# The pair of tiles that GpSimd stores: tiles 8 and 15 behind its second turn, or tiles 0 and 7 behind its first

## The chip, the cores and the metric

The kernel runs on one core of one Trainium2 chip. A core has five engines with instruction streams of their own (TensorE, VectorE, ScalarE, GpSimd, SyncE, in the profile PE, DVE, ACT, POOL, SP) and sixteen DMA engines. The metric is the time of one execution on the device in microseconds, as the median of several runs.

## The reference

```python
# x: (16, 512, 1024), weight: (1024, 768), add_value: (16, 512, 768), all float32; scale: 0.1
return (scale * np.matmul(x, weight) + add_value).astype(np.float32)
```

Flattened, this is one product of 8192 x 1024 by 1024 x 768, scaled, with an 8192 x 768 matrix added. The core reads x (32 MB), the weights (3 MB) and the added matrix (24 MB) and writes 24 MB.

## The kernel before

**Tiles and slots.** The 8192 rows are 64 tiles of 128 rows. Partition p of a block of 16 tiles holds 16 consecutive rows of the matrix, one for each tile, so that several tiles of one block are one contiguous piece of memory in each partition. x is loaded into `xs`, which has 16 slots of a tile each. `ao` has 32 slots: a tile of the added matrix is loaded there, the result overwrites it, and it is stored from there. Tile t uses slot t modulo 32, so tiles 32 to 39 can be loaded only when tiles 0 to 7 have been stored.

**Moving and turning.** ScalarE and GpSimd run the same program, `mover`: each casts half of every group of four tiles from `xs` to bfloat16 in one of two buffers `va` (L167, eight casts of 32 partitions for four tiles and engine). One turn of its loop is the 16 tiles of `xs`, so there are four turns, of 32 casts each. For each of them it waits until the x tiles have landed and until VectorE has transposed what was in that buffer. VectorE transposes two tiles at a time from `va` to `xt` (L182), TensorE multiplies (L214), and VectorE scales the product, adds `ao` and writes the result to `ao`, again for two tiles (L191). VectorE's loop `group` takes eight tiles in a turn. Its semaphore `made` counts finished tiles (above a constant `MADE`), `by_act` and `by_pool` count the casts of ScalarE and GpSimd.

**SyncE's order.** All other transfers are issued by SyncE from a list written by hand, `STREAM`: entries (kind, first tile, number of tiles), with "w" for weights, "x" for x, "a" for the added matrix, "o" for a store, "a+" for a wait for an added load, and "pair" for the pair's rows. `sync_engine` goes through it in order and waits before each entry for what it needs: an x load (L116) for the casts that free its slots, an added load (L129) for the added load before it and, from tile 32 on, for the store that frees its slots, a store (L147) for the results. They all go to one queue, q1 in the profile. The last store, of tiles 60 to 63, stands behind the list (L257).

**The pair.** Two tiles of one block of eight are not stored with the others. 122 of their 128 partitions are stored by GpSimd in three DMAs (`BY_POOL`: partitions 117 to 121, 0 to 104 and 105 to 116), and the last six, 122 to 127, by SyncE (`BY_SP`), all at L93. GpSimd's DMAs go to a queue of their own, q0 in the profile. GpSimd issues them between two parts of its `mover`: after `TURN_AT` turns it waits for the results, issues the three DMAs and goes on with the other turns:

```python
mover(nc.gpsimd, nc.gpsimd.tensor_copy, 1, by_pool, pool_go, 0, TURN_AT)
nc.gpsimd.wait_ge(made, MADE + PAIR.stop)
for p, n in BY_POOL:
    store_pair(nc.gpsimd, p, n, aside_sem)
mover(nc.gpsimd, nc.gpsimd.tensor_copy, 1, by_pool, pool_go, TURN_AT, T // X_SLOTS - TURN_AT)
```

The added load that reuses the first of the pair's slots waits for both of the pair's semaphores, `pair_sem` and `aside_sem`.

Of the kernel before, what the change touches and what calls it, by code (L numbers as in the profile page):

```python
# [21 lines left out]
STREAM = [  # L22
# [5 lines left out]
]  # L28
FIRST, LAST = (0, 8), (60, 4)
PAIR, TURN_AT = slice(8, 16, 7), 2  # L30
BY_SP, BY_POOL = [(122, 6)], [(117, 5), (0, 105), (105, 12)]


# [259 lines left out]
```

## Time and profile before

| | us |
|---|---|
| median of 3 runs | 208.49 |
| lowest and highest | 208.33, 208.66 |
| the profiled execution | 209.46 |
| its span, from the first to the last instruction | 207.7 |

The profile is of one execution. Its span leaves out 1.76 us that lie around the instructions, and the whole took 0.97 us longer than the median. Rows of the timeline give start, duration, engine, line, operation and tiles, how many instructions were drawn together, and in brackets the idle time before and what ended it. Rows of DMA issues give the size and the median time from issue to landing. "DMA share" is the busy share of the sixteen DMA engines together.

### The profile page before, as it was taken

Reading aid. Unit: us, or ns where it says so; the run is one execution under the profiler, and the core shown is the slowest. Engines: PE = TensorE matmul, PEld = TensorE weight load, DVE = VectorE, ACT = ScalarE, POOL = GpSimd, SP = SyncE. Lnnn points to the kernel's source line nnn. Section 1 sums busy time; section 2 is a strip of 40 time slices with the busy share of each in tenths; the row PEclk is TensorE's granted clock in tenths of the full one; section 3 lists DMA queues with packets and bytes.
Section 4 is the critical chain, followed back from the end, with each engine's and each line's share of the span. In section 5 each row is a group of like instructions: output and inputs, shape, how many; then the busy total and the mean of one; then the engine's idle time right before and its main releaser. Section 6 shows DMA issues by size and latency. Waiting matters only on the chain.

```text
span 207.7 us, 2223 instructions
## 1 busy us (share of the span) xinstructions
PE 167.7 (81%) x1008; PEld 50.4 (24%) x512; DVE 98.0 (47%) x66; ACT 134.7 (65%) x129; POOL 137.7 (66%) x135
## 2 busy tenths in 40 slices
PE   0000099999999999999999999999999997999800
PEld 0000023333333333333333333323332232333200
DVE  0005525537555555475555553855551934455310
ACT  2049970799999708999997069999990299900000
POOL 0049994799999907999999359999991199910000
PEclk9999999999999999999999999999999999999975
DMA  7999999999999999999999999999999999998983
GB/s 297 410 380 473 417 447 404 454 454 404 404 454 454 404 448 454 380 426 414 445 419 449 407 451 454 404 428 436 445 431 417 423 447 450 454 454 381 447 379 166
DMA packets 4067, 87.04 MB, mean 419 GB/s; under 512 B 476, under 2 KB 476, under 8 KB 1122
## 3 DMA queue, kind: packets, MB, share of 16 engines
q1 hardware_dynamic: 3874, 86.28, 97.1%
q0 software_dynamic: 192, 0.75, 0.9%
q14 instruction: 1, 0.01, 0.0%
HBM read 61.87 MB, written 25.17 MB: 419 GB/s over the span
## 4 chain that ended last, share of the span: by engine, by line
PE 36%; DMA 29%; POOL 18%; ACT 5%; issue 4%; DVE 3%; SPq 0%; POOLq 0%; DVEq 0%; ACTq 0%
PE mm L214 36%; POOL va L167 17%; DMA xs<-in_x_dram 15%; DMA out_dram<-ao 14%; ACT va L167 5%; DVE xt L182 2%; POOL out_dram L93 1%; DVE ao L191 1%; SPq L129 0%; SPq L116 0%; DVEq L180 0%; POOLq L160 0%; POOLq L162 0%; POOLq L157 0%; DVEq L191 0%
## 5 line engine op out<-in xcount | busy, mean ns | idle before, releaser
L214 PE MATMUL mm<-w_bf,xt 128*128 128x256 bf16 (+1 forms) x1008 | 167.7, 327 | 28.6 <-DVE xt L182 27.7
L167 POOL CAST va<-xs 32x1024 bf16<-32x1024 f32 x128 | 135.5, 1059 | 44.8 <-DMA xs<-in_x_dram 37.4
L167 ACT CAST va<-xs 32x1024 bf16<-32x1024 f32 x128 | 133.4, 1043 | 46.0 <-DMA xs<-in_x_dram 43.0
L191 DVE SCALAR_TENSOR_TENSOR ao<-mm,ao 128x1536 f32 (+1 forms) x32 | 56.2, 1757 | 72.8 <-PE mm L214 68.2
L212 PEld LDWEIGHTS <-xt 128*128 128x128 bf16 x512 | 50.4, 98 | 145.4 <-issue 116.2
L182 DVE STREAM_TRANSPOSE xt<-va 128x1024 f32<-128x1024 f32 x32 | 39.5, 1236 | 9.2 <-POOL va L167 7.1
L175 DVE CAST w_bf<-ao 128x3072 bf16<-128x3072 f32 x2 | 4.5, 2251 | 18.2 <-DMA ao<-in_weight_dram 18.2
L156 ACT ACT_TABLE_LOAD x1 | 1.3, 1283 | 1.3 <-SPq L246 1.3
L93 POOL DMA_DIRECT2D out_dram<-ao x3 | 2.0, 662 | 0.0
L274 POOL MEMSET const-float32-0.0<- 128x1 f32 x1 | 0.1, 98 | 0.2 <-issue 0.2
L274 POOL MEMSET const-bfloat16-1.0<- 128x1 bf16 x1 | 0.1, 101 | 0.0
L274 POOL MEMSET const-float32-1.0<- 128x1 f32 x1 | 0.1, 98 | 0.0
L274 POOL MEMSET const-uint8-127<- 128x1 uint8 x1 | 0.1, 98 | 0.0
## 6 DMA issues: line engine op xcount, KB each, us to landing
xs<-in_x_dram SPq DMA_DIRECT2D x7, 4096.0 KB, 22.3
ao<-in_add_value_dram SPq DMA_DIRECT2D x6, 3072.0 KB, 16.1
out_dram<-ao SPq DMA_DIRECT2D x3, 3072.0 KB, 29.1
ao<-in_add_value_dram SPq DMA_DIRECT2D x1, 6144.0 KB, 24.2
out_dram<-ao SPq DMA_DIRECT2D x1, 6144.0 KB, 31.8
out_dram<-ao SPq DMA_DIRECT2D x1, 4608.0 KB, 15.3
xs<-in_x_dram SPq DMA_DIRECT2D x2, 2048.0 KB, 21.0
ao<-in_weight_dram SPq DMA_DIRECT2D x2, 1536.0 KB, 16.9
```

The lines of the kernel that those rows point to most:

```text
L93: eng.dma_start(out_v[p:p + n, 0, PAIR, :], ao[p:p + n, PAIR, :]).then_inc(sem, 16)
L156: eng.preload_act_table(mybir.ActivationFunctionType.Copy)
L167: copy(va[q % VA_BUFS][32 * b:32 * b + 32, :, a, :], src[32 * a:32 * a + 32, :, b, :]).then_inc(count, 1)
L175: eng.tensor_copy(w_bf[:, s:s + n, :], ao[:, W_AT + s:W_AT + s + n, :]).then_inc(casts, n)
L182: eng.transpose(xt[:, 2 * half:2 * half + 2, :, :].rearrange("p i c m -> p (i c m)"), va[move % VA_BUFS][:, q:q + 2 * KC, :, :].bitcast(fp ...
L191: eng.scalar_tensor_tensor(a, mm[:, q:q + 2, 0:N], float(scale), a, op0=mybir.AluOpType.mult, op1=mybir.AluOpType.add).then_inc(made, 2)
L212: eng.ldweights(x_j, tile_position=(0, 0))
L214: m = eng.add_instruction(mybir.InstMatmult(start_tensor_calc=(j == 0), stop_tensor_calc=(j == KJ - 1), tile_size=(P, P), tile_position=(0 ...
L274: nc = _bacc.Bacc("TRN2", target_bir_lowering=False, num_devices=1)
```

## The change

Three constants change, no function:

```diff
 STREAM = [
...
-    ("x", 32, 8), ("a+", 16, 16), ("o", 0, 8), ("o", 9, 6), ("pair", 8, 8), ("a", 32, 8), ("x", 40, 8),
+    ("x", 32, 8), ("a+", 16, 16), ("pair", 0, 8), ("o", 1, 6), ("o", 8, 8), ("a", 32, 8), ("x", 40, 8),
...
-PAIR, TURN_AT = slice(8, 16, 7), 2
+PAIR, TURN_AT = slice(0, 8, 7), 1
```

The pair is now tiles 0 and 7. GpSimd's first part is one turn (tiles 0 to 15) instead of two, it then waits for tile 7 instead of tile 15, issues the same three DMAs, and does the other three turns. SyncE stores the pair's last six partitions first, then tiles 1 to 6, then tiles 8 to 15, where it stored tiles 0 to 7, then 9 to 14, then the pair's six partitions. The waits on the pair's two semaphores move from the added load of tiles 40 to 47 to that of tiles 32 to 39. The bytes, the sizes of the DMAs and their partitions are the same. GpSimd's first part has three register instructions less, as a loop of one turn has constants to wait for; the other engines' instructions are unchanged.

## The prediction

> **What bounds the kernel now.** I read the page first: the totals by engine, the 40 slices, and the queues.
>
> ```profile
> span 207.7 us, 2223 instructions
> PE 167.7 (81%) x1008; PEld 50.4 (24%) x512; DVE 98.0 (47%) x66; ACT 134.7 (65%) x129; POOL 137.7 (66%) x135
> DMA  7999999999999999999999999999999999998983
> DMA packets 4067, 87.04 MB, mean 419 GB/s; under 512 B 476, under 2 KB 476, under 8 KB 1122
> q1 hardware_dynamic: 3874, 86.28, 97.1%
> q0 software_dynamic: 192, 0.75, 0.9%
> ```
>
> TensorE looks like the busiest engine at 81%, but the DMA row is 9 in nearly every slice, and SP's queue (q1) and GpSimd's queue (q0) together fill 98.0% of the sixteen DMA engines' span. So I asked for stretches, for the time around the change and behind it (the last two columns are the DMA share and the rate):
>
> ```profile
> core 0: us, PE busy (x) PEld busy (x) DVE busy (x) ACT busy (x) POOL busy (x), PEclk, DMA share, GB/s
> 55.00:79.00 24.00, 23.84 (x147) 7.19 (x75) 13.73 (x10) 16.47 (x17) 16.80 (x18) 1.00 0.99 427
> 96.00:116.00 20.00, 19.90 (x123) 5.97 (x61) 11.42 (x8) 16.55 (x16) 18.92 (x20) 1.00 1.02 437
> 116.00:198.00 82.00, 78.24 (x474) 23.48 (x240) 44.20 (x30) 50.05 (x48) 49.77 (x48) 1.00 1.00 430
> ```
>
> The DMA engines are full in the stretch where GpSimd's stores run now (96 to 116), in the one where they would run (55 to 79) and in all that follows. The rate is not lower where the two queues share the engines: 437 GB/s against 427 and 430. The end of the kernel is therefore the bytes divided by the rate, as long as the queue never runs empty. Then I looked at the end itself, with SP's issues in order of time and the DMA engines' last 2 us (slices of 0.05 us):
>
> ```profile
> 160.44 27.70 SPq L147 DMA_DIRECT2D out_dram<-ao  x2
> 198.45 0.33 SPq L257 DMA_DIRECT2D out_dram<-ao  x1
> out_dram<-ao SPq DMA_DIRECT2D x1, 1536.0 KB, 8.3
> GB/s 0 0 0 0 0 0 246 0 0 0 0 0 0 0 0 246 0 0 0 0 0 0 0 0 246 0 0 0 0 0 0 0 0 0 0 0 0 0 0 0
> DMA packets 8, 0.04 MB, mean 18 GB/s; under 512 B 5, under 2 KB 5, under 8 KB 5
> ```
>
> The last store (L257) is issued at 198.45 and lands 8.3 us later, at 206.7. Its 1.57 MB at 430 GB/s need 3.7 us, so some 4.6 us of it are the queue ahead of it and latency, which this row doesn't part; I take a little under half, 2 us, as the slack that TensorE's end still has. In the last window, 204.7 to 206.7, only three data packets of 12 KB start, 0.46 us apart: one of the sixteen DMA engines is finishing alone, 1.5 us after the others. Both facts come back below.
>
> **The change part by part.** The profiled execution took 209.46 us with a span of 207.7 us; the median of three runs is 208.49 us, 0.97 us less. I make the sum on the span and carry its difference to the median.
>
> GpSimd's three stores move from behind its second turn to behind its first. Its rows and SP's issues:
>
> ```profile
> 37.63 35.04 POOL L167 CAST va<-xs 32x1024 bf16<-32x1024 f32 x32 [4.21 <-DMA xs<-in_x_dram]
> 78.92 17.49 POOL L167 CAST va<-xs 32x1024 bf16<-32x1024 f32 x16 [6.24 <-DMA xs<-in_x_dram]
> 96.36 1.98 POOL L93 DMA_DIRECT2D out_dram<-ao  x3
> 98.39 17.48 POOL L167 CAST va<-xs 32x1024 bf16<-32x1024 f32 x16
> 121.42 8.72 POOL L167 CAST va<-xs 32x1024 bf16<-32x1024 f32 x8 [5.55 <-DMA xs<-in_x_dram]
> 55.21 17.88 SPq L116 DMA_DIRECT2D xs<-in_x_dram  x2
> 73.27 0.82 SPq L147 DMA_DIRECT2D out_dram<-ao  x2
> 74.14 0.38 SPq L93 DMA_DIRECT2D out_dram<-ao  x1
> 96.00 0.36 SPq L129 DMA_DIRECT2D ao<-in_add_value_dram  x1
> 96.49 0.85 SPq L116 DMA_DIRECT2D xs<-in_x_dram  x1
> 115.23 0.33 SPq L129 DMA_DIRECT2D ao<-in_add_value_dram  x1
> 115.94 0.33 SPq L116 DMA_DIRECT2D xs<-in_x_dram  x1
> 48.86 1.76 DVE L191 SCALAR_TENSOR_TENSOR ao<-mm,ao 128x1536 f32 x1 [1.13 <-PE mm L214]
> ```
>
> 1. GpSimd's new wait. Tiles 8 to 15 are the first half of the run that starts at 37.63, so the first turn ends at 37.63 + 17.5 = 55.1. The wait is for tile 7, and VectorE finishes tiles 6 and 7 at 48.86 + 1.76 = 50.6, the fourth result of its first group. The wait costs nothing; the 1.98 us of issue do: casts of tiles 16 to 23 end at 74.7 instead of 72.7.
>
> 2. Who waits for that. SP loads x tiles 32 to 39 when GpSimd has moved tile 23; that issue (the second of the two from 55.21, which end at 73.1), and the pair and the stores behind it in SP's order, go 1.98 us later, to 74.7. The x load before it is still running until 78.9, so the queue has 4 us of work left and nothing idles: 0 us. If it were empty, this would cost 1.98 us.
>
> 3. The bytes of q0 come earlier. The three DMAs carry 732 KB:
>
> ```profile
> out_dram<-ao POOLq DMA_DIRECT2D x1, 630.0 KB, 15.1
> out_dram<-ao POOLq DMA_DIRECT2D x1, 72.0 KB, 17.3
> out_dram<-ao POOLq DMA_DIRECT2D x1, 30.0 KB, 7.5
> ao<-in_add_value_dram SPq DMA_DIRECT2D x6, 3072.0 KB, 16.1
> 87.77 1.25 DVE L182 STREAM_TRANSPOSE xt<-va 128x1024 f32<-128x1024 f32 x1 [0.75 <-POOL va L167]
> 90.46 1.76 DVE L191 SCALAR_TENSOR_TENSOR ao<-mm,ao 128x1536 f32 x1 [1.45 <-PE mm L214]
> ```
>
> That is 0.75 MB; at 427 GB/s, 1.75 us that lie ahead of the landing of x tiles 24 to 31. Casts of tile 24 then start at 80.7 instead of 78.9. The transpose of tiles 24 and 25, at 87.77 now, already waits for GpSimd; it moves to 89.5 and ends at 90.8. TensorE needs it when tile 23 is done, just before VectorE's 90.46. So TensorE gets a stall of about 0.4 us that it does not have now. If the DMA engine that is last brings 1 of its 1.5 us to this place too, it is 1.4 us. From below the term is 0, if most of q0's packets still stand behind that x load.
>
> The Trainium skill bears on that last point: DMA: Bandwidth & Descriptors, Queues, rings and completion order, says that a DMA engine alternates between its queues packet by packet. The rows fit it: 192 packets, 12 per engine, took 15 to 17 us to land where their bytes need 1.75 us. By that rule q0's packets would alternate with the packets of a 6144 KB load, twice as long, so that an estimate from it is some 25 us instead of 17 for the landing, and up to a third of the 1.75 us would fall behind the x load. The stall would then be 0 to 0.4 us, and the sum the same.
>
> 4. Where the stall goes. TensorE's own gaps:
>
> ```profile
> 26.09 137.03 PE L214 MATMUL mm<-w_bf,xt 128*128 128x512 bf16 x819 [26.09 <-DVE xt L182]
> 163.35 10.57 PE L214 MATMUL mm<-w_bf,xt 128*128 128x512 bf16 x63 [0.24 <-DVE xt L182]
> 175.32 20.98 PE L214 MATMUL mm<-w_bf,xt 128*128 128x512 bf16 x126 [1.40 <-DVE xt L182]
> 160.39 1.76 DVE L191 SCALAR_TENSOR_TENSOR ao<-mm,ao 128x1536 f32 x1 [4.62 <-DMA ao<-in_add_value_dram]
> ```
>
> It idles 0.24 and 1.40 us late in the run, and VectorE waits 4.62 us for an add load there: DMA sets the pace. A stall of 0.4 to 1.4 us at tile 24 only shortens these 1.64 us. Behind that stand the 2 us of slack at the end. So 0 us.
>
> 5. GpSimd's second turn no longer issues, which gives the 1.98 us back: casts of tile 32 follow those of tile 31 at once, 80.7 + 17.5 = 98.2 against 98.39 now, and end at 115.7. The x load that SP issues at 115.94 for it stays there. The x load at 96.49 waits for tile 31 and goes to 98.2, where the store of tiles 8 to 15 keeps the queue full for some 4 us. 0 us.
>
> 6. SP's order. Ahead of the add load at 96.00 stood one store of 3072 KB; now 36 + 732 + 2304 = 3072 KB stand there, so it is issued at the same time. It now carries the waits on both pair semaphores, but q0's packets, issued from 55.1 to 57.1, land near 74 with the 17.3 us of now and have until 96. The next add load, at 115.23 now, waits today for GpSimd's 72 KB DMA (issued as the last of three, at 97.8, landing 17.3 us later, at 115.1). That wait goes; the next one is the landing of the add load before it, near 96.0 + 16.1 = 112. The load is issued 3 us earlier but stands behind an x load that lands at 121.4 either way: 0 us.
>
> Bytes, packet sizes and rate are unchanged, the queue is never empty, and both stalls are covered. The sum is 0.0 us: **208.5 us**.
>
> **The rivals.** First, faster: the engine that ends alone. One engine of sixteen has 1.5 us more work, and the pair's rows are the only transfer that isn't spread evenly by size; the slow landing of q0 and the pair's DMAs on the same engines are a place where it could pick that up. If it meets them at another point and half of the lag disappears, the end is 0.7 us earlier: 207.8 us. If all of it does, 207.0. For it speaks that this tail alone sets the end; against it, that the same rows go to the same queues in the same shares.
>
> Second, slower: the same engine falls further behind. If its lag of 1.5 us at 206.4 grows with the time since GpSimd issued its stores (96.4, so 110 us), then an issue 41 us earlier makes it 1.5 x 151 / 110 = 2.1 us: 209.1 us. It decides from the first 0.4 us of added lag, as nothing covers the last engine. The same section's page has a rule of this kind: under Latency and other measured facts the Trainium skill says that two of the engines are usually slower, at a best guess through the rings of the software queue. No view of this trace tells one engine from another before the end, so I can neither confirm nor exclude it.
>
> Third, also slower: the x load of tiles 24 to 31 lands so late that the stall reaches the end. TensorE has 1.4 us at tile 24, 1.64 us in its gaps and 2 us at the end, so this decides from 5 us of delay, and at 6 us gives 209.5 us. The bytes make 1.75 us, and 2.8 us with the lag, so it needs q0 to hold the engines up by more than its bytes, which the 437 GB/s of 96 to 116 speaks against.
>
> **How the numbers follow.** No change has 0.40, with a range of its own of 208.1 to 208.9; the faster rival 0.27; the second 0.20; the third 0.13. The three runs differ by 0.33 us, so 0.2%, 0.4 us, is about what a measurement can tell from none. The two slower rivals lie beyond it, and so does the faster one, which makes the chances 0.27 faster, 0.40 within and 0.33 slower. The range reaches from 207.6, a little past half the lag, to 209.4, just short of the third.
>
> **What would show it.** Right: GpSimd's three DMAs start near 55.1, its casts of tile 24 near 80.7, SP's add load near 96, the wait of the transpose at 88 grows by about 1.8 us, TensorE's two late gaps shrink by as much as the new one, and the last store is issued near 198.4 and lands near 206.7. Wrong: a tail of one engine much shorter or longer than 1.5 us, a DMA share below 0.95 in 72 to 100, or a last store issued after 200.5.

## The result, and the profile after

| | before | changed |
|---|---|---|
| median of 14 runs, us | 208.50 | 209.28 |
| lowest and highest, us | 208.28, 208.66 | 208.43, 210.0 |
| the profiled execution and its span, us | 209.46, 207.7 | 209.5, 207.7 |

The changed kernel is slower: the ratio of the times is 1.0028, with an interval of 1.0017 to 1.0039, which is 0.6 us (the medians lie 0.8 us apart). It also scatters more, over 1.6 us instead of 0.4. The kernel before isn't free of such executions: of 80 more that were run beside the experiments, 10 took over 209 us, up to 209.61, where none of the 14 above did. Of the changed kernel's 14 it is 8. The forecast was 208.5 us with a range of 207.6 to 209.4, so the time lies inside the range, but outside the 208.1 to 208.9 that the forecast of no change gave itself: it is near where the second rival had it (209.1 us).

The first thing to see is that the two profiled executions have the same span of 207.7 us, so the difference of the medians is not in this pair of profiles at all. The profiled execution of before was 0.97 us above its median, the one of the changed kernel only 0.2 us above its own. A comparison of these two alone would have said "same".

The rows that answer to the prediction's steps come first. GpSimd's timeline of the changed kernel (start, duration, engine, line, operation, count, and the idle time before with what ended it):

```profile
37.54 17.47 POOL L167 CAST va<-xs 32x1024 bf16<-32x1024 f32 x16 [4.23 <-DMA xs<-in_x_dram]
54.96 1.98 POOL L93 DMA_DIRECT2D out_dram<-ao  x3
56.99 17.46 POOL L167 CAST va<-xs 32x1024 bf16<-32x1024 f32 x16
81.01 35.01 POOL L167 CAST va<-xs 32x1024 bf16<-32x1024 f32 x32 [6.57 <-DMA xs<-in_x_dram]
```

SyncE's timeline of the changed kernel, from the issue behind the change to the last store:

```profile
55.10 19.76 SPq L116 DMA_DIRECT2D xs<-in_x_dram  x2
75.04 0.35 SPq L93 DMA_DIRECT2D out_dram<-ao  x1
75.45 0.95 SPq L147 DMA_DIRECT2D out_dram<-ao  x2
96.26 0.34 SPq L129 DMA_DIRECT2D ao<-in_add_value_dram  x1
98.57 0.34 SPq L116 DMA_DIRECT2D xs<-in_x_dram  x1
110.96 0.33 SPq L129 DMA_DIRECT2D ao<-in_add_value_dram  x1
116.10 0.33 SPq L116 DMA_DIRECT2D xs<-in_x_dram  x1
198.97 0.33 SPq L257 DMA_DIRECT2D out_dram<-ao  x1
```

TensorE's timeline of the changed kernel, in which the runs are the time between its gaps:

```profile
25.98 64.81 PE L214 MATMUL mm<-w_bf,xt 128*128 128x512 bf16 x378 [25.98 <-DVE xt L182]
91.16 83.37 PE L214 MATMUL mm<-w_bf,xt 128*128 128x512 bf16 x504 [0.37 <-DVE xt L182]
175.85 20.97 PE L214 MATMUL mm<-w_bf,xt 128*128 128x512 bf16 x126 [1.32 <-DVE xt L182]
```

Every step of the sum is there. GpSimd issues at 54.96 without waiting and loses 1.98 us; the x load of tiles 32 to 39 ends its issue at 74.86; the casts of tile 24 start at 81.01 (80.7 was forecast); TensorE, whose late gaps before were 0.24 and 1.40, has the new stall of 0.37 us at 91 (0.4) and gives it back in its later gaps; the add load goes out at 96.26, the x load behind tile 31 at 98.57 (98.2), the next add load at 110.96 (112). The last store goes out later than forecast, at 198.97 instead of 198.4; the first experiment comes back to that. In stretches (busy time of each engine, granted clock, DMA share, rate), again of the changed kernel:

```profile
55.00:79.00 24.00, 23.84 (x147) 7.24 (x74) 14.20 (x10) 16.20 (x16) 18.50 (x20) 1.00 1.01 436
79.00:96.00 17.00, 16.58 (x102) 4.95 (x51) 8.70 (x6) 14.79 (x15) 14.21 (x14) 1.00 0.98 415
96.00:116.00 20.00, 19.90 (x123) 6.00 (x62) 11.73 (x8) 18.57 (x18) 18.92 (x19) 1.00 1.03 442
116.00:198.00 82.00, 79.09 (x481) 23.78 (x243) 43.71 (x30) 50.05 (x48) 49.73 (x49) 1.00 1.00 429
```

The DMA share is 0.98 to 1.03 everywhere, as forecast. So the time went to none of the places that the sum looked at. What is left is the end, which the sum took over unchanged.

**How the end is read.** The DMA view of one window, cut in 40 slices of 0.05 us, shows a packet's bytes in the slice where it starts. Here are 204.2 to 206.2 us of the changed kernel:

```profile
GB/s 0 0 0 0 246 0 0 492 0 0 0 0 0 0 0 0 492 0 0 0 0 0 0 0 0 246 0 0 0 0 0 0 0 0 246 0 0 0 0 0
```

and of a second profiled execution of the kernel before, which took 208.31 us with a span of 206.5 us:

```profile
GB/s 983 246 0 246 0 246 0 246 0 246 0 0 0 0 0 0 0 0 0 0 0 0 0 0 0 0 0 0 0 0 0 0 0 0 0 0 0 0 0 0
```

In the first, the last 12 KB packet starts in slice 34, at 205.9 us; in the second in slice 9, at 204.65. The spans are 1.8 and 1.85 us more than that. This holds for every kernel below, with 1.7 to 1.9 us: the last packet of the last DMA engine sets the span, and one engine is alone for as long as single packets stand some 0.45 us apart. This second execution of the kernel before, 0.2 us under its median, has no such tail. The tail of 1.5 us that the prediction was built on was a property of that one execution, which took 1 us more than its kernel's median.

I also followed the packets engine by engine. The records don't name the engine, so I joined each packet's start to the end of a packet before it, which gives sixteen chains; the assignment is my own working, and no view prints it. It holds together: in every trace each chain gets the same number of packets of each of SyncE's large transfers. In these chains no engine has a gap of over 0.4 us between 1.8 and 204 us in any kernel but one (rows last, below), and the median engine ends between 204.5 and 204.9 us in each kernel that the table further down lists. Only the last engine differs. That is the quantity to explain.

### The profile page after: what moved, and what is told of

Read it like the earlier page. It is cut to its first block, busy times and chain, and to the rows that moved or that the text cites. A ratio compares the mean times of both kernels' runs of the same rounds, so it can differ in the third digit from the quotient of the medians.

```text
span 207.7 us, 2219 instructions
## 1 busy us (share of the span) xinstructions
PE 168.3 (81%) x1008; PEld 50.5 (24%) x512; DVE 97.9 (47%) x66; ACT 134.7 (65%) x129; POOL 137.5 (66%) x135
## 4 chain that ended last, share of the span: by engine, by line
DMA 38%; POOL 23%; PE 16%; ACT 8%; issue 6%; DVE 4%; DVEq 0%; POOLq 0%; ACTq 0%; SPq 0%
DMA xs<-in_x_dram 38%; POOL va L167 23%; PE mm L214 16%; ACT va L167 8%; DVE xt L182 3%; DVE ao L191 1%; DVEq L180 0%; POOLq L160 0%; POOLq L162 0%; POOLq L157 0%; DVEq L206 0%; ACTq L160 0%; DVEq L191 0%; DVEq L188 0%; SPq L100 0%
```

## The experiments

The theories, by the letters that the expectations use as they came up: A, the transfers of the changed kernel make one DMA engine late; B, the moment at which GpSimd's code is fetched does it (the q14 row, a DMA of 8 KB on one engine); C, TensorE's path; D, the add load of tiles 40 to 47 that now goes out at 110.96 instead of 115.23; E, what q0's rows do where the stores turn into loads near 101 us; F, that any other place of GpSimd's code than that of the kernel before is worse; G, the place of SyncE's six rows. An edit "on before" or "on the changed kernel" says which of the two it starts from.

### 1. Again, and GpSimd's code alone, the pair's wait, no pair

The changed kernel a second time:

> The changed kernel once more, for a second trace and a second interval. Theory A (the transfers: what is slower is one DMA engine that ends later than the other fifteen, because the pair's rows meet it at another point): 209.1 us again, and a tail of one engine of 1 to 2 us before the last landing. Theory B (GpSimd's code: its second loop starts at another place and runs three turns, so its instructions are loaded at other moments): 209.1 us as well. Theory C (TensorE's path: the stall at tile 24 reaches the end): 209.1 us, with the last store issued 0.5 us or more later than 198.45 and no tail of one engine.

Measured: 209.18 us (208.44 to 209.62), ratio 1.0027 (1.0013 to 1.0042), the same as in the result. Its profiled execution happened to be its shortest, 208.44 us and a span of 206.6. TensorE's timeline there:

```profile
91.16 83.38 PE L214 MATMUL mm<-w_bf,xt 128*128 128x512 bf16 x512 [1.16 <-DVE xt L182]
174.84 20.98 PE L214 MATMUL mm<-w_bf,xt 128*128 128x512 bf16 x128 [0.31 <-DVE xt L182]
```

This execution has the larger stall at tile 24, 1.16 us, and ends 1.1 us earlier than the one with 0.37 us. One sign of C did show in the result's trace, a last store issued 0.52 us later than before (198.97 against 198.45), but the tail of one engine that C excluded was there too, and here the store is issued as follows:

```profile
197.97 0.33 SPq L257 DMA_DIRECT2D out_dram<-ao  x1
```

In my chains of both, every engine goes on into the packets of that store without a pause, so its issue holds nothing up. TensorE's path (C) is out.

The second kernel is the kernel before with GpSimd's first two turns written as two loops of one turn. It makes the same transfers at the same moments; only the program is longer.

```diff
-        mover(nc.gpsimd, nc.gpsimd.tensor_copy, 1, by_pool, pool_go, 0, TURN_AT)
+        mover(nc.gpsimd, nc.gpsimd.tensor_copy, 1, by_pool, pool_go, 0, 1)
+        mover(nc.gpsimd, nc.gpsimd.tensor_copy, 1, by_pool, pool_go, 1, 1)
```

> The kernel before, with GpSimd's first loop of two turns written as two loops of one turn: its code changes place and the second loop starts later in it, the transfers and their order do not change. Theory A: 208.5 us, with the spread of the kernel before (0.4 us). Theory B: 209 us or so, and a wider spread, as in the changed kernel. Theory C: 208.5 us.

Measured: 209.14 us (208.48 to 209.67), ratio 1.0030 (1.0015 to 1.0044): as slow as the changed kernel, without any of its transfers. What moved is the fetch of GpSimd's code. The queues of the kernel before in the stretch 96 to 116, and of this one in 75 to 96 (packets, MB, share of the sixteen engines):

```profile
q1 hardware_dynamic: 368, 7.98, 92.9%
q0 software_dynamic: 192, 0.75, 9.2%
q14 instruction: 1, 0.01, 0.1%
```

```profile
q1 hardware_dynamic: 355, 8.76, 99.1%
q14 instruction: 1, 0.01, 0.1%
```

The one q14 packet starts at 105.6 us in the kernel before, at 82.8 here and at 67.1 in the changed kernel. The expectation of B was met, so B seemed as good as A at this point.

The third kernel is the changed one with SyncE's six rows behind both stores, where the kernel before has them:

```diff
-    ... ("pair", 0, 8), ("o", 1, 6), ("o", 8, 8), ("a", 32, 8), ...
+    ... ("o", 1, 6), ("o", 8, 8), ("pair", 0, 8), ("a", 32, 8), ...
```

> The changed kernel with SyncE's six rows stored behind tiles 8 to 15 instead of ahead of tiles 1 to 6; GpSimd is left as in the changed kernel. Theory A, if SyncE's rows are what meets the late engine: 208.5 us; if GpSimd's rows are: 209.1 us. Theory B: 209.1 us. Theory C: 209.1 us.

Measured: 212.2 us (212.1 to 212.53), ratio 1.0179 (1.0166 to 1.0192), which no theory had expected. SyncE's timeline and the stretches of this kernel:

```profile
76.04 0.38 SPq L93 DMA_DIRECT2D out_dram<-ao  x1
103.41 0.36 SPq L129 DMA_DIRECT2D ao<-in_add_value_dram  x1
103.87 0.37 SPq L116 DMA_DIRECT2D xs<-in_x_dram  x1
```

```profile
96.00:116.00 20.00, 20.00 (x125) 5.97 (x61) 11.73 (x8) 18.52 (x18) 18.84 (x19) 1.00 0.90 373
```

The add load of tiles 32 to 39 waits for the pair's rows, these now stand behind the store of tiles 8 to 15, and it goes out at 103.41 instead of 96.26. The x load behind it is late with it, the queue runs dry (DMA share 0.90 where it was 1.03), and 0.13 x 20 us = 2.6 us of transfer time are missing; the time is 2.9 us above the changed kernel's 209.28. So the six rows can't have their old place together with the new wait; this run shows what that wait costs uncovered, and tells nothing on A or B.

The fourth is the kernel before without a pair: GpSimd does its four turns in one loop and stores nothing, SyncE stores tiles 8 to 15 whole, and the waits on the pair are gone.

```diff
-    ... ("o", 0, 8), ("o", 9, 6), ("pair", 8, 8), ("a", 32, 8), ...
+    ... ("o", 0, 8), ("o", 8, 8), ("a", 32, 8), ...
...
-        mover(nc.gpsimd, nc.gpsimd.tensor_copy, 1, by_pool, pool_go, 0, TURN_AT)
...
-        mover(nc.gpsimd, nc.gpsimd.tensor_copy, 1, by_pool, pool_go, TURN_AT, T // X_SLOTS - TURN_AT)
+        mover(nc.gpsimd, nc.gpsimd.tensor_copy, 1, by_pool, pool_go)
```

> The kernel before without the pair: SyncE stores tiles 0 to 7 and 8 to 15 whole, GpSimd issues nothing and runs its four turns in one loop. All results are stored. Theory A: the software queue's rows are no longer taken from anywhere, so every DMA engine has the same bytes; if one engine is slower by itself, it ends last by more than now, 209 to 210 us, and if the rows of GpSimd are what makes one late, 207.5 us. Theory B: below 208.5 us, as one loop starts at one place. Theory C: 208.5 us or a little less, as GpSimd saves its 2 us of issue.

Measured: 209.57 us (209.48 to 209.86), ratio 1.0053 (1.0040 to 1.0066), in five runs with hardly any scatter. Its queues:

```profile
q1 hardware_dynamic: 3856, 87.03, 98.0%
```

There is no q0 and no q14, all bytes go one way, and still it is 1 us slower than before. In my chains one engine is 3% slower than the others on stores (0.940 against 0.912 us for a packet of 24 KB) and equal on loads; here it ends 1.6 us behind the median. In the kernel before, q0 gives one engine 2 data packets of 6 KB where the others get 8, and that is the slow engine: the pair takes 6 x 0.234 = 1.4 us off it. By this working that is what the pair is worth, and its shares are the same at either place.

### 2. The add load, and GpSimd's code moved in both kernels

The changed kernel, in which SyncE holds back the add load of tiles 40 to 47 until the x load behind it can go too:

```diff
+                if s == 40:
+                    need(by_act, 80)
+                    need(by_pool, 80)
```

> The changed kernel, with the add load of tiles 40 to 47 held back until ScalarE and GpSimd have moved tile 39, which the x load behind it waits for anyway: it is issued near 115.8 us again, as in the kernel before, instead of 110.9. Theory D (the order in SyncE's queue: the add load that is issued 4 to 5 us earlier, now that it has no wait for GpSimd's stores, changes what the DMA engines meet when they go over from x tiles 48 to 55 to the stores, near 135 us, and one of them ends later): 208.5 us and a spread of 0.4 to 0.6 us, no packets longer than usual at 135. Theory B (the moment at which GpSimd's code is loaded): 209.2 us and a spread over 1 us.

Measured: 209.38 us (208.59 to 209.67), ratio 1.0034 (1.0020 to 1.0048). SyncE's timeline of it shows the load back at its old moment (the added lines move it to L132):

```profile
98.53 0.34 SPq L116 DMA_DIRECT2D xs<-in_x_dram  x1
116.09 0.33 SPq L132 DMA_DIRECT2D ao<-in_add_value_dram  x1
```

Nothing came back, so D is out.

Then the place of GpSimd's program in both kernels. `addr_align` sets where the code of an engine begins on a grid of 64 instructions; the offset is 4 in both. With 32 instead, the fetch comes at 46.5 us in the changed kernel and at 42.2 us in the kernel before, and no transfer changes:

```diff
-        eng.addr_align(HALF_BLOCK, offset=PAST, max_nops=0)
+        eng.addr_align(HALF_BLOCK, offset=32 if eng is nc.gpsimd else PAST, max_nops=0)
```

> The changed kernel with GpSimd's code placed 28 instructions later against the 64-instruction grid it is aligned to, so that its one load of code on the way (67.1 us in the changed kernel, 105.6 in the kernel before, 82.8 with the split loop) falls into its first turn, near 47 us. Transfers unchanged. Theory B: 208.5 us with a narrow spread if an early load is harmless. Theory D: 209.2 us with a spread over 1 us.

> The kernel before with the same move of GpSimd's code: its load of code falls near 47 us instead of 105.6. Theory B, if it is the moment of that load that matters: not 208.5 us, but nearer 209.1 us, if early is bad, or up to 0.4 us below 208.5, if it only takes the load away from the DMA engine that ends last. Theory D: 208.5 us.

> The kernel before once more, for a second trace, since the first one was of an execution 1 us above its median. Theories B and D: a span near 206.7 us, the code load near 105.6 us, a tail of one DMA engine under 1 us, no long packets at 135 us.

Measured: the changed kernel 209.44 us (208.62 to 210.08), ratio 1.0040 (1.0023 to 1.0057); the kernel before 209.22 us (208.74 to 210.15), ratio 1.0029 (1.0013 to 1.0045); the unchanged kernel before, looked at once more, 208.31 us with the short tail shown above. So the kernel before loses some 0.6 us by the ratio when only its code moves, a second time after the split loop, and the changed kernel's interval overlaps with the one that it had. B is a real cost, but it wasn't yet shown to be the changed kernel's.

### 3. No fetch on the way

With a grid of 128 and the offset 4, GpSimd's code is fetched at 1.8 us, as the first loads start, and never again. The first kernel is the changed one with this, the second has the offset 68, which leaves its fetch at 67 us:

```diff
-        eng.addr_align(HALF_BLOCK, offset=PAST, max_nops=0)
+        eng.addr_align(*((2 * HALF_BLOCK, 4) if eng is nc.gpsimd else (HALF_BLOCK, PAST)), max_nops=0)
```

> The changed kernel with GpSimd's code aligned to a grid of 128 instructions at offset 4 (64 and 4 before; a load of code brings 8 KB, which is 128 instructions of 64 bytes). Of this and the next kernel one should have its load of code on the way as the changed kernel has (67.1 us), the other none. With it: 209.2 us. Without it, by theory B: 208.5 us or less, with a narrow spread; if the load of code is not the cause of the changed kernel's time: 209.2 us and a spread over 1 us all the same.

> The same with offset 68: the other half of the pair. The one of the two that has no load of code between 2 and 200 us tells the theories apart: 208.5 us or less by theory B, 209.2 us if other causes hold.

Measured: 209.42 us (209.16 to 209.53), ratio 1.0048 (1.0035 to 1.0061) without the fetch, 209.30 us (208.78 to 209.67), ratio 1.0040 (1.0025 to 1.0054) with it. Taking the fetch away brings nothing, so the moment of the fetch isn't why the changed kernel is slower. Its transfers are (A), and B is a second cost that happens to have about the same size.

### 4. The fetch taken out of the kernel before, and its rows first

The kernel before with the grid of 128 and the offset 4 (same edit as above), and the kernel before in which only SyncE's six rows go ahead of the stores, as in the changed kernel:

```diff
-    ... ("o", 0, 8), ("o", 9, 6), ("pair", 8, 8), ("a", 32, 8), ...
+    ... ("pair", 8, 8), ("o", 0, 8), ("o", 9, 6), ("a", 32, 8), ...
```

> The kernel before with GpSimd's code aligned to the 128-instruction grid at offset 4, the place at which the changed kernel had its load of code at the very start (1.8 us) and none later. Transfers unchanged. Theory B (in the kernel before it is the moment of the code load that matters, 105.6 us being a cheap one): with no load on the way 208.2 to 208.5 us with a narrow spread. Theory F (any other place of GpSimd's code is worse, for a reason other than this load): 209.2 us and a spread over 1 us, as with the split loop and the moved code.

> The kernel before with SyncE's six rows of tiles 8 and 15 stored ahead of the two large stores, as the changed kernel has it, and not behind them. GpSimd's part and its code are those of the kernel before. Theory E (what the changed kernel loses is that GpSimd's rows no longer stand among the packets when the DMA engines go over from the second store to the add load, near 101 us): 208.5 us. Theory G (it is the place of SyncE's six rows): 209.2 us.

Measured: without the fetch 208.35 us (208.10 to 208.76), ratio 0.9985 (0.9973 to 0.9997), the fastest kernel of this study, which takes F out: another place is not worse if it holds no fetch on the way. With the rows first 209.05 us (208.34 to 209.54), ratio 1.0017 (1.0000 to 1.0034). The last 2 us (204.2 to 206.2) of the former and of the latter:

```profile
GB/s 0 492 737 737 492 246 492 737 0 0 0 492 0 0 0 0 246 0 0 0 0 0 0 0 0 0 0 0 0 0 0 0 0 0 0 0 0 0 0 0
```

```profile
GB/s 246 983 492 492 0 246 0 0 0 246 0 0 246 0 0 0 0 0 0 0 0 246 0 0 0 0 0 0 0 0 246 0 0 0 0 0 0 0 0 0
```

The former's last packet starts at 205.0 us (span 206.8), the latter's at 205.7 (span 207.5), behind lonely packets as in the changed kernel. One edit in the order of SyncE's list, with GpSimd's three stores left at 96 us and the pair left at 8 and 15, adds 0.5 us to the median where the whole change adds 0.8. That is nearer to G than to E, whose condition, GpSimd's rows at the turn near 101 us, is still met here. Its interval begins at 1.0000, so by times alone it is at the edge of what can be told from none. The scatter doesn't help, as the kernel before reached 209.54 us too on the chip of this pair of runs: 6 of 12 executions with the rows first are over 209 us, 4 of 23 of the kernel before.

**Where the late engine loses its time.** In my chains, packets that take longer than their kind stand at a few fixed moments. For the engine that ends last, the extra time in us at each of them (the fetch counts its own packet and the packet behind it):

| kernel, time of this execution | behind the median at the end | fetch | near 101 | near 136 | near 175 |
|---|---|---|---|---|---|
| before, 208.31 | 0.50 | 0.4 | 0 | 0 | 0 |
| before, 209.46 | 1.80 | 0.4 | 0.4 | 0 | 0.7 |
| before, no fetch on the way, 208.63 | 0.58 | 0 | 0 | 0 | 0 |
| before, fetch at 42.2, 209.36 | 1.56 | 0.7 | 0 | 0 | 0.5 |
| before, rows first, 209.28 | 1.45 | 0 | 1.0 | 0.3 | 0.6 |
| changed, 208.44 | 0.69 | 0 | 0.4 | 0.6 | 0 |
| changed, 209.5 | 1.92 | 0 | 0.8 | 1.2 | 0.1 |
| changed, no fetch on the way, 209.16 | 1.57 | 0 | 0.5 | 0.8 | 0.5 |

Near 101, stores turn into loads; near 136, loads into stores; near 175, again loads into stores. (At the turn at 85 to 88 us most engines have long packets in nearly all traces, mostly 0.2 to 0.9 us in the kernel before and 0.15 to 0.5 in the changed one; they are left out here, as most engines share them.) In all six traces with the changed kernel's transfers, rows last aside, an engine loses 0.2 to 0.8 us near 101, and the same one 0.5 to 1.2 us near 136. In five of them this is the engine that ends last; in the changed kernel with its code moved, the last one is the engine that took the fetch, with 0.7 us. With the rows first it is 1.0 and 0.3. In all seven the long packet near 101 is the last large store packet of its engine before the add load; in the kernel before, no large store packet is long there. In the five traces of the kernel before with its own order, whatever its code, there is 0 to 0.4 near 101, at a packet of the six rows, and nothing near 136. The loss near 175 stands only at engines that are 0.7 us or more behind by then, and not at all of these. The one last engine that loses 0.4 us by the fetch and no more ends 0.5 us late; those with a second loss end 1.4 us late or more.

## Why the prediction was right or wrong

**What bounds the kernel** was right as far as the DMA engines go. All kernels that keep the queue full end within 1.3 us of each other, and the only one that lets it run dry (rows last) pays for it at once.

**Steps 1, 2, 4, 5 and 6** were right in their times, most within 0.4 us, the second add load of step 6 within 1.1, and in their price of 0. (Step 6 let q0's packets land near 74 us, as before; they were slower and landed near 78, which 96 still covers.) Holding the earlier add load back changes nothing, as step 6 had it. Step 6 looked at the cover of the new wait for q0's packets alone; the same load also waits for SyncE's six rows, and rows last shows what that costs without cover, 2.9 us.

**Step 3** was right in the stall and in q0's slower landing. The DMA issues of the changed kernel from 55 to 79 us:

```profile
out_dram<-ao POOLq DMA_DIRECT2D x1, 630.0 KB, 19.7
out_dram<-ao POOLq DMA_DIRECT2D x1, 72.0 KB, 21.6
```

The Trainium skill's rule (DMA: Bandwidth & Descriptors, Queues, rings and completion order), that an engine alternates packet by packet, gave some 25 us against the 15 to 17 of before; 20 to 22 were measured, so the trace agrees with its direction, and in the chains q0's packets do stand mostly one by one between the load's packets.

**The step that failed** is the last sentence of the sum, "Bytes, packet sizes and rate are unchanged, the queue is never empty, and both stalls are covered", with the sum of 0.0 us behind it. Each part of it is true, and the 0.0 us doesn't follow. The end isn't bytes by rate but the end of the last of sixteen engines, and the mean rate can't show an engine that loses 0.5 us more than the others: that is 0.03 us of the mean. The sum has no term for the last engine: it took the lag of 1.5 us as fixed, and so the term as nothing. That the range held the result all the same is due to the rivals that widened it. Measured, the lag is 0.5 us in an execution of the kernel before near its median, 1.8 in the one that the sum was made on, and 0.7 and 1.92 us in two of the changed kernel.

**The second rival** had the right place, the right threshold ("nothing covers the last engine") and the right price, 209.1 against 209.28. Its mechanism was wrong, so the price came by luck. It made the lag grow with the time since GpSimd's stores; but the two executions of the kernel before issue these at the same time and differ by 1.3 us in the lag, and rows first leaves them at 96 us and loses 0.5 of the 0.8 us. The lag comes in lumps, at the fetch and at the turns between loads and stores. The Trainium skill's best guess (DMA: Bandwidth & Descriptors, Latency and other measured facts), that engines are slower through the rings of the software queue, has the kernel without the pair against it here: that kernel has no packets on a software queue, and its slow engine is slow all the same, on stores alone.

**The first rival** (the lone engine is relieved) did not come, though its premise was right: the pair's rows are what unloads that engine, and since the change keeps their shares, it keeps the relief. **The third** needed 5 us of delay at tile 24; 0.37 to 1.16 us came.

**Shown:** the loss is in the changed kernel's transfers, not in TensorE, the early add load or the code fetch; and the last engine's end sets the span, its last packet starting 1.7 to 1.9 us before it in every trace. **Likely, not shown to the end:** that it is the six rows ahead of the stores. Rows first gives 0.5 of 0.8 us at the edge of its interval, with long packets at the same turns. **Open:** why a packet on one engine takes 0.2 to 0.9 us longer at a turn, and why less so with the six rows behind the stores; whether GpSimd's early stores add to it, or the order of the two large stores, which the change swaps as well (six tiles, then eight) and no run tried alone. The changed kernel with its rows behind the stores would part the rows from the rest, but there the new wait costs 2.9 us and covers it.

## What to carry to other kernels

In a kernel that keeps all DMA engines full, the span is the end of the last engine. Read it in slices of the last 2 us, find out in more than one execution how far that engine is behind, and put it in the sum as a term with a range, for a change to the order of transfers can move it. Before comparing two profiles, hold each against its kernel's median: here the one of before was 1 us above its own and hid the whole effect. And when a change of program makes a kernel slower, try the same change with the transfers left alone: here a fetch of code at another moment cost some 0.6 us by itself.

The fastest version is not the changed kernel but the one before with GpSimd's code on a grid of 128 instructions: 208.35 us, ratio 0.9985 (0.9973 to 0.9997).

## What the runs showed of the hardware

- One fetch of GpSimd's code, 8 KB on one engine in some 208 us, moves the end of this kernel, whose DMA engines are full: 208.50 us with it at 105.6 us, 209.14 and 209.22 with it at 82.8 and 42.2, 208.35 without it on the way.
- In the chains, one of the sixteen engines takes 0.940 us for a store packet of 24 KB where the others take 0.912, and no longer for a load. Without the pair this engine ends last, and the kernel is 1 us slower (209.57 us, five runs within 0.4); with it another engine does in all of these traces but rows last.
- At the turns between loads and stores single packets take up to 0.9 us longer on one engine, and it doesn't catch up. The two traced executions of the changed kernel, 208.44 and 209.5 us, differ by this; untraced ones lie between 208.43 and 210.0.
